# Two layers of a hybrid gMLP, S5 and pooling backbone on one core: where modulation loads, first splits, lag rows and outputs stand in the queues

## The chip, the core and the metric

One core of one Trainium2 chip runs the whole program, and the metric is device microseconds of one execution. In the profile PE is TensorE (PEld its weight loads), DVE VectorE, ACT ScalarE, POOL GpSimd and SP the engine that only issues DMAs. Each engine works through its instructions in order, and a DMA queue belongs to the engine that issues it. The profile comes from one more execution than the timed ones.

## The reference

There are 512 latent tokens, 256 context tokens, a width of 1024 and two layers. Layer 1 returns latent tokens only. Cut to what matters here:

```python
for i in range(2):
    mod = silu(c) @ w_mod[i] + b_mod[i]          # for c (latent) and c_ctx (context)
    sh1, sc1, g1, sh2, sc2, g2 = split(mod, 6)
    h = rms_norm(x, norm_mix_pre[i]) * (1 + sc1) + sh1
    z = h @ w_in[i]                              # 1280 columns: 512 gMLP, 512 S5, 256 pooling
    a = spatial_gating(z[:, :512])
    s = glu(gelu(d * u + sum over 2 directions of Re(C scan(lam, B u))))   # u = z[:, 512:1024]
    p = pool_mixer(z[:, 1024:])                  # means over 2, 4, 8 and 16 tokens
    x = x + g1 * rms_norm(concat(a, s, p) @ w_out[i], norm_mix_post[i])
    h = rms_norm(x, norm_ffn_pre[i]) * (1 + sc2) + sh2
    x = x + g2 * rms_norm((silu(h @ w_gate[i]) * (h @ w_up[i])) @ w_down[i], norm_ffn_post[i])
```

x starts as the input plus a fixed sine and cosine table. The S5 part has 32 groups of 16 channels and 64 complex states, and runs over context and latent tokens in both directions.

## The kernel before

The work is tiled by 128 tokens (six tiles, of which the first two are context). Products with large weights are made of three: each weight block and each activation is split into a rounded part and a rest (`split`, line 130: ScalarE casts, VectorE subtracts), and `mm3` (line 141) issues rounded by rounded, rounded by rest and rest by rounded. `wblock` (line 134) loads a 512 KB block through SP's queue into one of two buffers `raw` and splits it into `whi` and `wlo`.

*Order.* The program is written as Python generators. A planner places the instructions on the engines: an earlier line has the higher priority, an instruction goes to its engine when the planner's own clock holds it ready, and a buffer is given out when an older tile of its tag is released. `tc.issue_after(ins)` puts the instructions made within its block, on the engine of `ins`, behind `ins`. `tc.high_priority` raises a block.

*Prologue* (lines 1224 to 1299). Small vectors go through ScalarE's queue (`dmas`, lines 1230 to 1250), x and ctx through SP. `first_mod_loads` (192) loads the parts of `w_mod` that layer 0's first shift and scale need, 16 pieces of 512 KB (some as 1 MB), by column quarters j; between its first pieces and the rest `prep_load_rows` (494) loads B as rows and C. For each j `first_mod_sums` (212) forms the sums on TensorE, `first_mod` (221) makes the columns, with the bias in `fbias`, and `to_hT` (339) makes a quarter of the transposed input h in three token pairs and splits it. `ssm_params` (363) is the discretization, a long chain of small VectorE instructions with two ScalarE sines; its last TensorE transposes are on line 441.

*Block preparation* `ssm_prep` (513). For each eight groups (layer 0) or four (layer 1) it makes rotation tables Td, state inputs X, their reversed copy XF (line 597) turned to Ed, outputs Y and their reversed copy (line 629) written as Fd, and the lag matrix Kd (line 674 on). All five are written to device memory through GpSimd's queue. In layer 0 it runs one step at a time (`bgstep`) beside the first weight products; layer 1's runs in the FFN of layer 0.

*Mixing* (853). `z_B` (866) makes the S5 inputs u of 128 channels each, m = 0 to 3. Then `PRE_A` steps of the gMLP product follow, then eight blocks bt of the recurrence. A block has `ssm_UV` (769, products with E), `ssm_rot` (794, two scans on VectorE between two rotations) and `ssm_y` (824, products with T and F). `ssm_FT` (782) loads F, and for every second block T, in eight pieces of 64 KB that are shifted windows of Kd. `ssm_y` writes its result to device memory (`yd`) and at once fetches it back transposed, in four loads. All of these are on SP's queue. Between the blocks `fl` gives steps of the gMLP and pooling products, and `filler` steps of the modulations.

*Modulations.* `mod_rows` (232) forms one 1024-wide part on TensorE: a bias product, then eight steps of one 512 KB load (tag `rawm`, two buffers, SP) and four products. `mod_rows_v` (255) does it on VectorE with accumulators per lane (latent, context), then a bias product and one product per lane. In layer 0's mixing run (0, 3), (0, 4), (0, 2) and (0, 5), the number being the sixth of `w_mod`. In the FFN of layer 0 run layer 1's six by `mod_rows_v`: `filler` (1323) takes one step after an up block and two in a down block, and the rest ahead of the last down part.

Of the kernel before, what the change touches and what calls it, by code (L numbers as in the profile page):

```python
# [84 lines left out]
def tile_backbone(ctx, tc, A, out):  # L85
# [39 lines left out]

    last_v = [None]
# [65 lines left out]
    def first_mod_loads(res):  # L192
# [4 lines left out]
        for (j, m), w in where.items():  # L197
# [5 lines left out]
            else:  # L203
                res[j, m] = []
                for h in range(2):
                    t = wp.tile([128, 4, 256], F32, tag=w, name=nm("wm"), bufs=2)
                    dma(t, A["w_mod"][0, 512 * h:512 * h + 512, c_].rearrange("(t p) c -> p t c", p=128))
# [23 lines left out]

    def mod_rows(l, m, res):
        ps = mdt()
        bm = wp.tile([1, 1024], F32, name=nm("bm"), tag="rawm", bufs=2)
        dma(bm, A["b_mod"][l:l + 1, m * 1024:(m + 1) * 1024])
        for j in range(4):
            mm(ps[32 * j:32 * j + 32, :256], bc(ident[0:1, 0:1], [1, 32]),
               bm[:, 256 * j:256 * j + 256], start=True, stop=False, tile_position=(0, 32 * j))
        for k in range(8):
            raw = wp.tile([128, 1024], F32, name=nm("wm"), tag="rawm", bufs=2)  # L240
            dma(raw, A["w_mod"][l, k * 128:(k + 1) * 128, m * 1024:(m + 1) * 1024])
            for j in range(4):
                mm(ps[32 * j:32 * j + 32, :256], csil[:, 2 * k:2 * k + 32], raw[:, 256 * j:256 * j + 256],
                   start=False, stop=k == 7, tile_position=(0, 32 * j))
            if k % 2 == 1:
                yield
        M = sp.tile([128, 256], F32, tag="M", name=nm("M"), bufs=1)
        S.copy(M, ps[:, :256])
        res.append(M)

# [4 lines left out]
    def mod_rows_v(l, m, res, lanes):  # L255

        accs = [q4([128, 1024], s="macc") for _ in range(lanes)]
        for k in range(8):
            raw = wp.tile([128, 1024], F32, name=nm("wm"), tag="rawm", bufs=2)
            dma(raw, A["w_mod"][l, k * 128:(k + 1) * 128, m * 1024:(m + 1) * 1024])  # L260
# [7 lines left out]
        bm = wp.tile([1, 1024], F32, name=nm("bm"), tag="rawm", bufs=2)  # L268
        dma(bm, A["b_mod"][l:l + 1, m * 1024:(m + 1) * 1024])
        ps = mdt()  # L270
        for j in range(4):
            c_ = slice(256 * j, 256 * j + 256)
            mm(ps[32 * j:32 * j + 32, :256], bc(ident[0:1, 0:1], [1, 32]), bm[:, c_], start=True, stop=False,
               tile_position=(0, 32 * j))
# [1092 lines left out]
```

## Time and profile before

| | us |
|---|---|
| three runs | 1552.45, 1559.03, 2079.58 (median 1559.03) |
| profiled execution | 1553.79 |
| its span, from the first to the last instruction | 1552.0 |
| TensorE busy in it | 1475.9 |

Busy time of a stage says how full an engine is there. A wait counts only where the waiting engine has nothing else, and above all TensorE. The stages of the profiled execution are the prologue to about 66 us, the first products with layer 0's preparation to 160, its recurrence to 285, output projection to 400, FFN to 960, then layer 1: mixing to 1200, FFN to the end.

### The profile page before, as it was taken

Reading aid. Unit: us, or ns where it says so; the run is one execution under the profiler, and the core shown is the slowest. Engines: PE = TensorE matmul, PEld = TensorE weight load, DVE = VectorE, ACT = ScalarE, POOL = GpSimd, SP = SyncE. Lnnn points to the kernel's source line nnn. Section 1 sums busy time; section 2 is a strip of 40 time slices with the busy share of each in tenths; the row PEclk is TensorE's granted clock in tenths of the full one; section 3 lists DMA queues with packets and bytes.
Section 4 is the critical chain, followed back from the end, with each engine's and each line's share of the span. In section 5 each row is a group of like instructions: output and inputs, shape, how many; then the busy total and the mean of one; then the engine's idle time right before and its main releaser. Section 6 shows DMA issues by size and latency. Waiting matters only on the chain.

```text
span 1552.0 us, 22603 instructions
## 1 busy us (share of the span) xinstructions
PE 1475.9 (95%) x8777; PEld 1227.6 (79%) x8777; DVE 841.0 (54%) x1479; ACT 630.7 (41%) x1182; POOL 161.1 (10%) x281
## 2 busy tenths in 40 slices
PE   4899898999999999999999999999988999999996
PEld 3766695888888778888778887899778888888885
DVE  5977864646465676445763336587555332333334
ACT  3778564446323234233222215656454223222222
POOL 1113210012000010000010005211011000000003
PEclk9999999999999999999999999999999999999998
DMA  9788987773334455333674314768474333333332
GB/s 294 246 274 262 306 273 220 254 181 108 92 109 121 138 185 175 111 95 118 209 261 128 95 62 130 235 170 240 112 265 135 95 95 97 99 102 97 96 95 82
DMA packets 219487, 250.68 MB, mean 162 GB/s; under 512 B 41806, under 2 KB 164058, under 8 KB 218868
## 3 DMA queue, kind: packets, MB, share of 16 engines
q1 hardware_dynamic: 209268, 214.26, 45.5%
q0 software_dynamic: 9344, 34.58, 6.4%
q8 instruction: 69, 1.13, 0.3%
q10 hardware_dynamic: 768, 0.40, 0.1%
q14 instruction: 38, 0.31, 0.1%
HBM read 206.76 MB, written 42.43 MB: 161 GB/s over the span
## 4 chain that ended last, share of the span: by engine, by line
PE 81%; DMA 9%; DVE 4%; ACT 3%; POOL 1%; issue 1%; SPq 1%; DVEq 0%; POOLq 0%; ACTq 0%
PE acc L142 20%; PE acc L144 19%; PE acc L143 19%; PE aux L144 4%; PE aux L142 4%; PE aux L143 4%; PE pr L147 3%; PE md L147 3%; PE aux L147 2%; DMA F<-Fd 2%; DMA raw<-in_w_out_dram 1%; DMA wm<-in_w_mod_dram 1%; DVE w L132 1%; DMA raw<-in_w_in_dram 1%; PE acc L147 1%
## 5 line engine op out<-in xcount | busy, mean ns | idle before, releaser
L142 PE MATMUL acc<-h,w 128*128 128x512 f32 (+1 forms) x1248 | 430.1, 346 | 1.2 <-ACT w L131 0.8
L144 PE MATMUL acc<-h,w 128*128 128x512 f32 (+1 forms) x1248 | 428.4, 344 | 2.8 <-DVE w L132 2.8
L143 PE MATMUL acc<-h,w 128*128 128x512 f32 (+1 forms) x1248 | 429.5, 345 | 1.5 <-DVE h L356 1.4
L132 DVE TENSOR_TENSOR w<-raw,w 128x1024 fp32r<-128x1024 f32 x190 | 233.0, 1227 | 335.1 <-ACT w L131 332.3
L131 ACT CAST w<-raw 128x1024 fp32r<-128x1024 f32 x190 | 199.3, 1050 | 411.7 <-PE acc L143 231.3
L142 PEld LDWEIGHTS acc<-h,w 128*128 128x128 f32 x1248 | 235.8, 190 | 33.6 <-issue 3.4
L144 PEld LDWEIGHTS acc<-h,w 128*128 128x128 f32 x1248 | 236.1, 189 | 33.1 <-DVE w L132 3.6
L143 PEld LDWEIGHTS acc<-h,w 128*128 128x128 f32 x1248 | 236.3, 189 | 30.8 <-DVE h L356 2.3
L1142 DVE TENSOR_TENSOR fsg<-fsg,acc 128x512 f32<-128x512 f32 (+1 forms) x68 | 39.8, 585 | 159.7 <-PE acc L144 156.8
L144 PE MATMUL aux<-w,act 128*128 128x512 f32 x220 | 86.2, 393 | 0.0
L143 PE MATMUL aux<-w,act 128*128 128x512 f32 x220 | 86.2, 392 | 0.0
L144 PE MATMUL acc<-w,act 128*128 128x512 f32 x220 | 86.0, 391 | 0.0
L143 PE MATMUL acc<-w,act 128*128 128x512 f32 x220 | 85.8, 390 | 0.0
L142 PE MATMUL aux<-w,act 128*128 128x512 f32 x220 | 82.7, 390 | 0.0
L142 PE MATMUL acc<-w,act 128*128 128x512 f32 x220 | 82.5, 392 | 0.0
L266 DVE SCALAR_TENSOR_TENSOR macc<-wm,csil,macc 128x1024 f32<-128x1024 f32 x56 | 70.6, 1278 | 5.5 <-DMA wm<-in_w_mod_dram 5.4
L1143 ACT CAST act<-fsg 128x512 fp32r<-128x512 f32 (+1 forms) x68 | 36.5, 537 | 87.5 <-DVE fsg L1142 87.5
L1141 ACT ACTIVATE fsg<-acc 128x512 f32<-128x512 f32 (+1 forms) x68 | 34.8, 511 | 81.4 <-PE acc L144 81.4
L143 PE MATMUL acc<-w,h 128*128 128x512 f32 (+1 forms) x160 | 55.6, 348 | 1.1 <-DVE w L132 1.1
L147 PE MATMUL md<-wm,csil 128*32 128x256 f32 (+1 forms) x416 | 35.6, 404 | 21.1 <-DMA wm<-in_w_mod_dram 21.1
L144 PE MATMUL acc<-w,h 128*128 128x512 f32 (+1 forms) x160 | 55.2, 345 | 0.0
L142 PE MATMUL acc<-w,h 128*128 128x512 f32 (+1 forms) x160 | 53.9, 354 | 0.0
(370 smaller groups left out, 2322.8 us busy)
## 6 DMA issues: line engine op xcount, KB each, us to landing
wm<-in_w_mod_dram SPq DMA_DIRECT2D x90, 512.0 KB, 4.3
raw<-in_ffn_w_gate_dram SPq DMA_DIRECT2D x44, 512.0 KB, 3.9
raw<-in_ffn_w_up_dram SPq DMA_DIRECT2D x44, 512.0 KB, 3.8
raw<-in_ffn_w_down_dram SPq DMA_DIRECT2D x44, 512.0 KB, 3.8
raw<-in_w_in_dram SPq DMA_DIRECT2D x28, 512.0 KB, 5.0
raw<-in_w_out_dram SPq DMA_DIRECT2D x26, 512.0 KB, 6.9
xt<-xd SPq DMA_DIRECT2D x18, 512.0 KB, 4.9
Ed<-Et POOLq DMA_DIRECT2D x16, 512.0 KB, 4.7
```

The costliest lines, as they stand in the source:

```text
L131: S.copy(hi, raw)
L132: last_v[0] = V.tensor_sub(lo, raw, hi)
L142: PE.matmul(ps, lhi, rhi, start=start, stop=False, skip_group_check=True)
L143: PE.matmul(ps, lhi, rlo, start=False, stop=False, skip_group_check=True)
L144: return PE.matmul(ps, llo, rhi, start=False, stop=stop, skip_group_check=True)
L147: return PE.matmul(ps, lhsT, rhs, start=start, stop=stop, skip_group_check=True, **k)
L266: V.scalar_tensor_tensor(accs[r], raw, c_, accs[r], op0=ALU.mult, op1=ALU.add)
L1141: S.activation(sg[:, :n], p1[:, :n], AF.Silu)
L1142: V.tensor_mul(sg[:, :n], sg[:, :n], p2[:, :n])
L1143: S.copy(act[0][:, fl, o:o + n], sg[:, :n])
```

## The change

The diff, cut to its core (in both modulation functions the loads change from `dma`, SP, to `dmap`, GpSimd):

```diff
-    def wblock(src, shape, tags=("whi", "wlo")):
+    def wblock(src, shape, tags=("whi", "wlo"), after=()):
...
-        split(raw, hi, lo)
+        with ExitStack() as st:
+            for ins in after[:2]:
+                st.enter_context(tc.issue_after(ins.ins))
+            split(raw, hi, lo)
...
+    def bias_rows(l, m, lanes):
+        M = sp.tile([128, 256], F32, tag="M", name=nm("M"), bufs=1)
+        GP.memset(M, 0.0)
+        for r in range(lanes):
+            dmap(M[r:128:32, :], A["b_mod"][l, m * 1024:(m + 1) * 1024].rearrange("(j c) -> j c", j=4))
+        return M
...
     def mod_rows(l, m, res):
...
+        for k in range(0, 8, 2):
+            raw = [wp.tile([128, 1024], F32, name=nm("wm"), tag="rawm", bufs=2) for _ in range(2)]
+            for kk in range(2):
+                dmap(raw[kk], A["w_mod"][l, (k + kk) * 128:(k + kk + 1) * 128, m * 1024:(m + 1) * 1024])
+            if k == 2:
+                M = bias_rows(l, m, 2)
+            for kk in (1, 0):
+                for j in range(4):
+                    mm(ps[32 * j:32 * j + 32, :256], csil[:, 2 * (k + kk):2 * (k + kk) + 32],
+                       raw[kk][:, 256 * j:256 * j + 256], start=k == 0 and kk == 1, stop=k == 6 and kk == 0,
+                       tile_position=(0, 32 * j))
+            yield
+        V.tensor_add(M, ps[:, :256], M)
...
+    def prep_load_C(l):
         Cr = q4([128, 2, 4, 2, 64], s="Cr")
         for i, s_ in enumerate(("re", "im")):
-            dma(raw[32 * i:32 * i + 32], A[f"ssm_b_{s_}"][l].rearrange("k g a b -> g k (a b)"))
             for k in range(2):
                 dma(Cr[:, i, :, k, :], A[f"ssm_c_{s_}"][l, k].rearrange("(b g) h p -> (g h) b p", b=4))
-        return raw, Cr
+        return Cr
+
+    def prep_load_rows(l, raw):
+
+        for i, s_ in enumerate(("re", "im")):
+            dma(raw[32 * i:32 * i + 32], A[f"ssm_b_{s_}"][l].rearrange("k g a b -> g k (a b)"))
+        return raw
...
-        for i in range(2):
-            ps = prt()
+        with ExitStack() as st:
+            for ins in ssm["h", 2] if bufs is not None else ():
+                st.enter_context(tc.issue_after(ins.ins))
+            for i in range(2):
...
-                S.copy(XF[0:64, i], X[0:64, i, :, ::-1, :])
+                (GP.tensor_copy if l == 0 else S.copy)(XF[0:64, i], X[0:64, i, :, ::-1, :])
...
+                Kw[l, blk] = dr.tile([8, 16, 8, 128], F32, name=nm("Kw"))
...
-                S.copy(XF[64:128, i], Y[64:128, i, :, ::-1, :])
+                (GP.tensor_copy if l == 0 else S.copy)(XF[64:128, i], Y[64:128, i, :, ::-1, :])
...
+            if g0 % 8 + ng == 8:
+                for s in range(8):
+                    dmap(Kw[l, blk][s].rearrange("h g c -> g h c"), Kd[l, blk][:, :, 16 * (7 - s):16 * (7 - s) + 128])
...
-            for s in range(8):
-                dma(T_[16 * s:16 * s + 16], Kd[l, blk][:, :, 16 * (7 - s):16 * (7 - s) + 128]
-                    .rearrange("g h c -> h g c"))
+            dma(T_.rearrange("p g c -> p (g c)"), Kw[l, blk].rearrange("s h g c -> (s h) (g c)"))
...
-        dma(yd.rearrange("t h g c -> (t h) (g c)"), yt)
-        for g in range(4):
-            p0 = 64 * (bt % 2) + 16 * g
-            dma(g_[p0:p0 + 16, :, c0:], yd[:, :, g, :].rearrange("t h c -> h t c"))
+        ins = dma(yd.rearrange("t h g c -> (t h) (g c)"), yt)
+
+        def back():
+            for g in range(4):
+                p0 = 64 * (bt % 2) + 16 * g
+                dma(g_[p0:p0 + 16, :, c0:], yd[:, :, g, :].rearrange("t h c -> h t c"))
+
+        with tc.issue_after(ins.ins):
+            for f_ in late:
+                f_()
+        late[:] = [back]
+        if bt == 7:
+            late.clear()
+            back()
...
-            hi, lo = wblock(w_in[:, :, 512 + 128 * m:640 + 128 * m], [128, 8, 128])
+            hi, lo = wblock(w_in[:, :, 512 + 128 * m:640 + 128 * m], [128, 8, 128],
+                            after=ssm["h", min(m + 2, 3)] if l == 0 else ())
...
-        dmas(vrow[r0:r0 + w], s_)
-    dmas(dmask, A["k_dm"])
-    dmas(par01, A["k_par"])
+        dmap(vrow[r0:r0 + w], s_)
...
-    BC0 = prep_load_rows(0, pzb[0:64, 4:6])
+    brows = prep_load_rows(0, pzb[0:64, 4:6])
     drain(loads)
     next(params)
+    with tc.issue_after(ssm["wmod"].ins):
+        BC0 = brows, prep_load_C(0)
+        dma(dmask, A["k_dm"])
+        dma(par01, A["k_par"])
...
-    bg.append(ssm_prep(0, *BC0, bufs=pzb))
-    bgstep(6)
...
-            first_mod_sums(j, wm0, fps)
+            with ExitStack() as st:
+                if j == 0:
+                    st.enter_context(tc.issue_after(ssm["turned"].ins))
+                first_mod_sums(j, wm0, fps)
...
+            ssm["h", j] = last_s[0], last_v[0], last_h[0]
+    bg.append(ssm_prep(0, *BC0, bufs=pzb))
+    bgstep(6)
...
-            mods = chain(mod_cols(l, 3, 3, None), mod_cols(l, 4, 2, 16 + 8 * l), mod_G(l, 2), mod_G(l, 5))
+            mods = chain(mod_cols(l, 3, 3, None), mod_cols(l, 4, 2, 16 + 8 * l), mod_G(l, 2))
...
-            mq = chain(mod_cols(1, 0, 1, None, 2), mod_cols(1, 1, 0, 8, 2), mod_cols(1, 3, 3, None, 1),
+            mq = chain(mod_G(0, 5, 2), mod_cols(1, 0, 1, None, 2), mod_cols(1, 1, 0, 8, 2), mod_cols(1, 3, 3, None, 1),
```

Beside this, the memset and the four bias loads of `fbias` move behind the vector loads, onto GpSimd's queue. `mod_rows_v` takes its bias from `bias_rows` after its eighth step, so its first lane's product starts the sum in PSUM and VectorE adds the bias. `ssm["wmod"]` is the last load of `first_mod_loads`, `ssm["turned"]` the last transpose on line 441, and `ssm["h", j]` holds the last ScalarE, VectorE and TensorE instruction of quarter j of h.

## Rows read from the trace of the kernel before

**Rows 1.** The page: the span, and busy time, share and instructions of TensorE.

```profile
span 1552.0 us, 22603 instructions
PE 1475.9 (95%) x8777; PEld 1227.6 (79%) x8777; DVE 841.0 (54%) x1479; ACT 630.7 (41%) x1182; POOL 161.1 (10%) x281
```

**Rows 2.** Busy us by stage: PE, PEld, DVE, ACT, POOL (instructions); clock, DMA share, GB/s.

```profile
39.00:66.00 27.00, 21.92 (x250) 19.16 (x250) 26.61 (x68) 20.15 (x42) 2.54 (x5) 0.87 0.69 207
66.00:160.00 94.00, 94.00 (x684) 66.20 (x683) 71.73 (x230) 73.69 (x160) 21.35 (x41) 1.00 0.87 281
160.00:200.00 40.00, 33.51 (x266) 27.58 (x264) 35.13 (x69) 20.84 (x54) 11.88 (x13) 0.91 0.96 308
220.00:285.00 65.00, 58.25 (x441) 42.89 (x441) 34.74 (x48) 30.27 (x58) 2.63 (x4) 0.95 0.79 239
400.00:820.00 420.00, 420.00 (x2445) 345.57 (x2444) 248.75 (x406) 132.56 (x229) 27.86 (x50) 1.00 0.48 151
1040.00:1110.00 70.00, 64.75 (x492) 59.82 (x491) 46.18 (x81) 37.14 (x79) 6.93 (x10) 0.98 0.72 208
```

**Rows 3.** Timeline of TensorE, the first weight product: start, us, engine, line, operation, tiles.

```profile
66.82 0.36 PE L142 MATMUL acc<-h,w 128*128 128x256 f32 x1
```

**Rows 4.** Timelines of ScalarE and SP in the prologue.

```profile
16.50 0.26 ACT L402 ACTIVATE pwork<-pwork 128x64 f32<-128x64 f32 x1 [12.30 <-DMA cr<-in_sgu_b_dram]
...
17.93 1.94 SPq L500 DMA_DIRECT2D Cr<-in_ssm_c_re_dram  x2
22.04 0.92 SPq L500 DMA_DIRECT2D Cr<-in_ssm_c_im_dram  x2
```

**Rows 5.** VectorE's groups by line, 39 to 66 us: busy us, mean ns, idle before.

```profile
L356 DVE TENSOR_TENSOR h<-h,h 128x512 fp32r<-128x512 f32 x9 | 6.1, 681 | 0.0
L355 DVE CAST h<-h 128x512 fp32r<-128x512 f32 x9 | 3.8, 420 | 0.3 <-ACT h L351 0.2
L132 DVE TENSOR_TENSOR w<-raw,w 128x1024 fp32r<-128x1024 f32 x2 | 2.4, 1216 | 0.0
```

**Rows 6.** Timeline of TensorE, a bias, a k step and what follows.

```profile
171.93 0.63 PE L147 MATMUL md<-bm,ident 1*32 1x256 f32 x8
172.49 0.64 PE L147 MATMUL md<-wm,csil 128*32 128x256 f32 x8
173.06 1.58 PE L147 MATMUL aux<-zslot,E 128*128 128x96 f32 x12
```

**Rows 7.** TensorE's waits from 160 to 285 us: in total, times, longest.

```profile
PE md L147 <- DMA wm<-in_w_mod_dram: 6.1, 5, 2.2
PE pr L147 <- DMA pc<-in_k_pc_dram: 2.5, 1, 2.5
PE aux L147 <- DMA E<-Ed: 1.8, 1, 1.8
```

**Rows 8.** Timeline of SP in the recurrence of layer 0.

```profile
152.90 8.04 SPq L789 DMA_DIRECT2D T<-Kd  x8
188.35 3.37 SPq L841 DMA_DIRECT2D wk<-yd  x4
```

**Rows 9.** Groups by line and form: GpSimd's and ScalarE's copies; Kd's issue, and its landing.

```profile
L798 POOL COPY wk<-PT 128x384 f32<-128x384 f32 x16 | 19.6, 1226 | 94.8 <-DVE wk L807 94.6
L679 POOL DMA_DIRECT2D Kd<-klag x4 | 2.2, 557 | 13.9 <-DVE klag L669 13.8
...
L597 ACT COPY pz<-pz 64x1024 f32<-64x1024 f32 x8 | 8.0, 1043 | 0.3 <-DVE pz L550 0.3
...
Kd<-klag POOLq DMA_DIRECT2D x4, 120.0 KB, 5.3
```

**Rows 10.** VectorE's group of one modulation sum.

```profile
L266 DVE SCALAR_TENSOR_TENSOR macc<-wm,csil,macc 128x1024 f32<-128x1024 f32 x56 | 70.6, 1278 | 5.5 <-DMA wm<-in_w_mod_dram 5.4
```

**Rows 11.** Timeline of GpSimd, two of the copies of line 798.

```profile
164.10 0.50 POOL L798 COPY wk<-PT 128x384 f32<-128x384 f32 x1 [7.73 <-DVE wk L807]
184.86 5.00 POOL L798 COPY wk<-PT 128x384 f32<-128x384 f32 x1 [8.35 <-DVE wk L807]
```

More of the change, by code (lines that the diff above doesn't have):

```diff
@@ L206, in first_mod_loads @@
                     t = wp.tile([128, 4, 256], F32, tag=w, name=nm("wm"), bufs=2)
-                    dma(t, A["w_mod"][0, 512 * h:512 * h + 512, c_].rearrange("(t p) c -> p t c", p=128))
+                    ssm["wmod"] = dma(t, A["w_mod"][0, 512 * h:512 * h + 512, c_].rearrange("(t p) c -> p t c", p=128))
                     res[j, m] += [t[:, k] for k in range(4)]
@@ L230, in first_mod @@
                                bc(vecT[:, ks][:, None, :], [128, 2, 2]), op0=ALU.add, op1=ALU.mult)
+    def bias_rows(l, m, lanes):
[4 more added lines that the diff above has]
+        return M
     def mod_rows(l, m, res):
         ps = mdt()
[L234 to L248, printed above, removed]
+        for k in range(0, 8, 2):
[11 more added lines that the diff above has]
+        V.tensor_add(M, ps[:, :256], M)
         res.append(M)
@@ L259, in mod_rows_v @@
             raw = wp.tile([128, 1024], F32, name=nm("wm"), tag="rawm", bufs=2)
-            dma(raw, A["w_mod"][l, k * 128:(k + 1) * 128, m * 1024:(m + 1) * 1024])
+            dmap(raw, A["w_mod"][l, k * 128:(k + 1) * 128, m * 1024:(m + 1) * 1024])
             for r in range(lanes):
@@ L267, in mod_rows_v @@
             yield
-        bm = wp.tile([1, 1024], F32, name=nm("bm"), tag="rawm", bufs=2)
-        dma(bm, A["b_mod"][l:l + 1, m * 1024:(m + 1) * 1024])
+        M = bias_rows(l, m, lanes)
         ps = mdt()
[L271 to L274, printed above, removed]
         for r in range(lanes):
@@ L277, in mod_rows_v @@
                 mm(ps[32 * j:32 * j + 32, :256], osel[:, 31 - r:63 - r], accs[r][:, 256 * j:256 * j + 256],
-                   start=False, stop=r == lanes - 1, tile_position=(0, 32 * j))
-        M = sp.tile([128, 256], F32, tag="M", name=nm("M"), bufs=1)
-        S.copy(M, ps[:, :256])
+                   start=r == 0, stop=r == lanes - 1, tile_position=(0, 32 * j))
+        V.tensor_add(M, ps[:, :256], M)
         res.append(M)
@@ L440, in ssm_params @@
                 V.tensor_copy(dup, R[:, i:i + 1, :].to_broadcast([128, 2, 64]))
-                PE.transpose(ps[:, 128 * (i - b0):128 * (i - b0) + 128],
-                             dup.rearrange("p a b -> p (a b)"), ident)
+                ssm["turned"] = PE.transpose(ps[:, 128 * (i - b0):128 * (i - b0) + 128],
+                                             dup.rearrange("p a b -> p (a b)"), ident)
             pv = ps[:, :128 * (b1 - b0)].rearrange("p (i l k g) -> p i l k g", l=2, k=2, g=G)
@@ L529, in ssm_prep @@
              .rearrange("p a (g h) -> p a g h", h=16))
-        for i in range(2):
-            ps = prt()
-            for blk in range(4):
-                PE.transpose(ps[:, 128 * blk:128 * blk + 128], Cr[:, i, blk].rearrange("p k q -> p (k q)"), ident)
-            S.activation(Cc[:, i], ps, AF.Copy, scale=(1.0, -1.0)[i])
+        with ExitStack() as st:
+            for ins in ssm["h", 2] if bufs is not None else ():
+                st.enter_context(tc.issue_after(ins.ins))
+            for i in range(2):
+                ps = prt()
+                for blk in range(4):
+                    PE.transpose(ps[:, 128 * blk:128 * blk + 128], Cr[:, i, blk].rearrange("p k q -> p (k q)"), ident)
+                S.activation(Cc[:, i], ps, AF.Copy, scale=(1.0, -1.0)[i])
         yield
@@ L1232, in tile_backbone @@
     dmas(jrow, A["k_j"][:, None, :])
-    GP.memset(fbias, 0.0)
-    for m in range(2):
-        for hf in range(2):
-            c0 = 64 * m + 32 * hf
-            src = A["b_mod"][0:1, 1024 * m:1024 * m + 1024].rearrange("o (j h c) -> o h j c", j=4, h=2)[:, hf]
-            dmas(fbias[c0:c0 + 2], src.to_broadcast([2, 4, 128]))
     for n_, r0, w in (("norm_mix_pre", 0, 16), ("norm_ffn_pre", 16, 16), ("glu_b", 32, 8),
@@ L1247, in tile_backbone @@
             s_ = a_.rearrange("l (k p) -> (l k) p", p=128)
-        dmas(vrow[r0:r0 + w], s_)
-    dmas(dmask, A["k_dm"])
-    dmas(par01, A["k_par"])
+        dmap(vrow[r0:r0 + w], s_)
+    GP.memset(fbias, 0.0)
+    for m in range(2):
+        for hf in range(2):
+            c0 = 64 * m + 32 * hf
+            src = A["b_mod"][0:1, 1024 * m:1024 * m + 1024].rearrange("o (j h c) -> o h j c", j=4, h=2)[:, hf]
+            dmap(fbias[c0:c0 + 2], src.to_broadcast([2, 4, 128]))
     for h in range(2):
```

10 lines of the change are left out of this document (5 added, 5 removed).

## Prediction

> **What bounds the kernel now.** I read the page first, then busy time by stage, then the timelines and waits of the stages where TensorE is not full. The page shows TensorE busy for 1475.9 of 1552.0 us [rows 1]: the end is set by TensorE's work and by the gaps in it. The stages say where the gaps are [rows 2]. From 66 to 160 us, and in the FFN of layer 0 (400 to 820), TensorE is busy all the time: there only less TensorE work helps. Ahead of that, TensorE reaches the first weight product at 66.82 [rows 3], while VectorE is busy for 26.61 of the 27 us from 39 to 66 [rows 2]: until 66 it is VectorE that sets the pace. In the recurrence of layer 0 TensorE lacks 6.49 us from 160 to 200 and 6.75 from 220 to 285, at a mean granted clock of 0.91 and 0.95 (full, 2.4 GHz, with stretches at the half level, 1.2, where TensorE had waited), which costs another 0.09 x 40 = 3.6 and 0.05 x 65 = 3.3 us of full-clock work: 20.1 us lost there. The same stage of layer 1 (1040 to 1110) lacks 5.25 us. The DMA share is 0.79 to 0.96 in layer 0's recurrence.
>
> **The change part by part.** Durations are of the profiled execution (span 1552.0, run 1553.79); the sum starts from 1553.8. The median of the three runs shown is 1559.03, 5 us above; I expect a repeat near the profiled one.
>
> 1. *The start.* ScalarE's first sine waits 12.30 us behind its own queue of small loads [rows 4]; six vector loads and four bias loads go to GpSimd's queue, so the discretization chain on VectorE and the norms can start earlier, by those 12.30 us at most. GpSimd has idle time there; its ten issues, at the 0.557 us of a Kd issue [rows 9], are 5.6 us beside the loads of x. SP issues the C blocks between 17.93 and 22.96 [rows 4], ahead of most of w_mod; they move behind it, so the last quarter of w_mod can land up to 5.0 us earlier. The prologue's h work is 6.1 + 3.8 us on VectorE between 39 and 66, the two weight splits 2.4 [rows 5]; the other 14.3 of the 26.6 us are block preparation and small columns. Splits and preparation now stand behind h, on both engines by an added order. What queues behind a split is the first products; who waits is TensorE. The first weight product can come between 0 and 2.4 + 14.3 = 16.7 us earlier. I take 6.2: 5.0 for the C loads and one 1.2 us split. I don't take more, because the preparation put back is due again before the recurrence starts, and VectorE has 94 - 71.7 = 22.3 us left in 66 to 160 to hold it. Sum -6.2, ends 0 and -16.7.
>
> 2. *TensorE work.* One k step of a modulation on TensorE starts at 172.49, the next work at 173.06: 0.57 us; a bias (171.93 to 172.49) is 0.56 [rows 6]. The change drops the bias products of ten modulations, adding a memset and one or two small loads on GpSimd and a VectorE add in place of a ScalarE copy. Six of the ten are in the FFN, two in 66 to 160, where TensorE is full: 8 x 0.56 = -4.5. The modulation (0, 5) moves to the FFN as VectorE sums: 2 lanes x 0.57 = +1.1 us of TensorE there, and 16 sums at 1.278 us = 20.4 us of VectorE [rows 10], which is busy 248.75 of 420 there [rows 2]: room for it, 0 to +5, taken 0. The queue now ends the up and down steps with ten leftover steps instead of one; they run under the last down part. Sum -3.4, ends -4.5 and +1.6.
>
> 3. *The recurrence of layer 0.* There TensorE waits 6.1 us for w_mod, 2.5 for the pooling constants and 1.8 for E [rows 7]. All three come off SP's queue, which is in order: eight T loads hold it for 8.04 us at 152.90, and the four fetches of yd at 188.35 for 3.37, because they wait for yd to land [rows 8]. Four such T groups become one load each; fetches stand behind the next block's write and no longer wait; w_mod goes to GpSimd's queue; and 4.2 MB of w_mod (8 loads of 512 KB), some 17 us at the 239 GB/s of 220 to 285 [rows 2], leave for a stage with a DMA share of 0.48. The modulation that leaves also takes 8 x 0.57 + 0.56 = 5.1 us from TensorE, and two more biases 1.1. What is late next is VectorE's rotation, whose blocks are a chain, and the last fetch, which is unchanged. Ends: 0, and -(20.1 + 6.2) = -26.3. I take the waits named, 10.4, and half of the 6.9 us of clock: -13.9, and nothing for the TensorE work, since it lies in a stage that has gaps.
>
> 4. *The recurrence of layer 1.* The same T loads and fetches; lost are 5.25 us and 0.02 x 70 = 1.4 of clock. Ends 0 and -6.7; taken -4.0.
>
> 5. *GpSimd's load.* XF's two halves, 8 + 8 copies of 64x1024 in layer 0, leave ScalarE at 1.043 us each (the first eight in [rows 9]). The trace has no such copy on GpSimd; its 128x384 copies take 1.226 us on average [rows 9], 0.50 where nothing is in the way and 5.00 in one case [rows 11]. By length, 1024 for 384, that is 1.33 us at the 0.50 and 3.27 at the mean. At 1.33 the chain of preparation grows by 16 x 0.29 = 4.6 us, at 3.27 by 16 x 2.23 = 35.7; ScalarE gets back 16.7. Of Kw's eight copies per block, the first waits for Kd to land, 5.3 us, and each takes 0.557 to issue [rows 9]: up to 5.3 + 4.5 = 9.8 us of GpSimd per block, behind which stand the next block's XF copies, its writes and the w_mod pairs; TensorE waits for the last and for XF's turned tiles. Three blocks are in the way, ends 0 and +29. A Kd row is written late in a block, when the next block's first XF is due, so part of it can be met. I take +4.0 in all, nearest to the row of 0.50, because most of what preparation issues on GpSimd has slack up to the recurrence; ends -4, where only ScalarE's relief counts, and +36. By GpSimd's busy time, 21.35 of 94 us in 66 to 160 [rows 2], the change adds 16 x 1.33 = 21.3, three Kw groups 13.4 and some 16 w_mod issues 9: 65 of 94, still below full.
>
> The row of 5.00 us [rows 11] lies in the stretch where VectorE, with its products and sums of two tiles each, is busy 35.13 of 40 us [rows 2]. The Trainium skill (SBUF — State Buffer, section Who interferes with whom) has a rule that speaks against this edit: a VectorE instruction with two inputs in SBUF and a GpSimd instruction that reads SBUF lock each other out, and the later one waits for the whole of the other. The trace agrees in that row, ten times the 0.50 beside it. By the rule alone the copies would cost the +36, and the sum would be 1562; by the row of 0.50 it is the one below.
>
> Sum: -6.2 - 3.4 - 13.9 - 4.0 + 4.0 = -23.5, so **1530 us**.
>
> **The rivals.**
> - *More of the gaps close.* The first product comes the full 16.7 us earlier, the recurrence gives 20.1, layer 1 6.7, GpSimd costs nothing: -16.7 - 3.4 - 20.1 - 6.7 = -46.9, 1507 us. For it: every wait named in the recurrence comes from the queue that is emptied. Against it: VectorE is busy 35.13 of 40 us from 160 to 200 [rows 2], so the rotation soon sets the pace.
> - *The gains are hidden.* The preparation's end, not the first product, sets when the recurrence starts, and w_mod waits for GpSimd instead of SP: the wait stays and only changes its queue. Then 3.4 and 4.0 remain: 1546 us. For it: TensorE is already full from 66 to 160, so an earlier start only brings forward its fillers. Against it: TensorE's waits lie in the recurrence, behind SP.
> - *Slower: GpSimd's copies sit on the chain of preparation.* At 3.27 us a copy the chain grows by 35.7 us, the start's gain is swallowed by it, and 3.4 + 4.0 stay: 1553.8 + 35.7 - 7.4 = 1582 us. It decides from the copy's mean at which 16 x (t - 1.043) eats the sum of the other terms, 27.5: t = 2.76 us. For it: the mean of the GpSimd rows, and VectorE's load of 71.73 in 94 us. Against it: ScalarE, busy 73.69 of 94 [rows 2], gets time back, and the chain has TensorE's fillers beside it. The rule cited in part 5 gives the reason why it could come so.
> - *The change doesn't do what it says:* an order that the planner gives differently from the source (it places by priority, so a moved line need not move an instruction). That falls into the hidden case.
>
> **How the numbers follow.** Forecast (1514 to 1546): 0.50. More gaps close (1490 to 1514): 0.22. Hidden (1546 to 1560): 0.18. Slower (above 1560): 0.10, of which 0.06 above 1585. The bound of 2%, about what a measurement of this kernel can tell from no change, is 31 us: 1523 and 1585. Faster: 0.22 and 0.18 of the forecast's own half-range below 1523, 0.40; slower 0.06; same 0.54. The range leaves out 0.1 on either side: 1503 to 1560. The likeliest case's own range is 1514 to 1546.
>
> **What would show it.** Right: the first weight product before 62; C loads after the last w_mod issue; no TensorE wait on w_mod or the pooling constants between 160 and 285; one T issue per pair of blocks; granted clock near 1.0 from 160 to 285; XF copies near 1.3 us. Wrong: XF copies near 3 us, TensorE or the turned tiles waiting for them; TensorE waiting for w_mod on GpSimd's queue; VectorE without a gap and TensorE waiting for splits in the FFN of layer 0.

## The result, and the profile after

The changed kernel takes 1566.8 us (median) where the kernel before took 1554.5 in the same measurement. The ratio, which leaves out one run of the kernel before that was far slower than the rest (2079.58 us), is 1.0092 with a 95% interval of [1.0068, 1.0116]; the two medians by themselves give 1.0079. It is slower by 0.9%, less than the 2% bound. Forecast was 1530, range 1503 to 1560.

The page of the kernel after, against [rows 1]: TensorE is as busy as before, so the 13.6 us by which the profiled execution is longer are gaps. But it is as busy with 128 matmuls fewer: the mean granted clock over the span is 0.972, before it was 0.987.

```profile
span 1565.6 us, 22441 instructions
PE 1475.3 (94%) x8649; PEld 1235.8 (79%) x8649; DVE 872.7 (56%) x1505; ACT 613.8 (39%) x1158; POOL 280.1 (18%) x477
```

The windows of [rows 2], of the kernel after (columns as there):

```profile
39.00:66.00 27.00, 25.44 (x299) 21.97 (x299) 26.19 (x68) 20.52 (x49) 9.93 (x15) 1.00 0.76 227
66.00:160.00 94.00, 84.00 (x557) 58.59 (x556) 67.46 (x194) 49.02 (x110) 42.89 (x64) 0.96 0.80 257
160.00:200.00 40.00, 28.00 (x182) 20.53 (x183) 25.79 (x54) 17.55 (x48) 20.39 (x26) 0.54 0.80 252
220.00:285.00 65.00, 58.66 (x491) 51.32 (x491) 43.09 (x84) 35.88 (x83) 15.98 (x28) 0.94 0.75 242
400.00:820.00 420.00, 419.28 (x2447) 347.20 (x2446) 257.86 (x420) 134.77 (x232) 70.47 (x126) 1.00 0.47 141
1040.00:1110.00 70.00, 66.80 (x504) 63.54 (x504) 58.06 (x99) 40.13 (x92) 8.23 (x14) 0.96 0.74 230
```

Until 66 us TensorE gained (25.44 busy for 21.92). Then, from 66 to 160, where it had been full, it lacks 10 us; from 160 to 200 it lacks 12, and in these 40 us the granted clock is 0.54, near the half level of 1.2 GHz, after that waiting. VectorE and ScalarE are not the fuller for it: they have *less* to show from 66 to 160 (67.46 for 71.73, 49.02 for 73.69; up to 16.7 us of the latter are the copies that ScalarE gave away). Everybody waits.

Three milestones tell where. They are the first product of a rotation on VectorE: the first and the eighth of layer 0, and the first of layer 1. Kernel before, timeline of VectorE (start, us, engine, line, operation, tiles, idle time before it):

```profile
158.01 0.96 DVE L801 TENSOR_TENSOR wk<-zslot 128x768 f32<-128x768 f32 x1 [3.23 <-ACT zslot L779]
...
243.55 0.97 DVE L801 TENSOR_TENSOR wk<-zslot,tab 128x768 f32<-128x768 f32 x1
...
1013.32 0.95 DVE L801 TENSOR_TENSOR wk<-zslot 128x768 f32<-128x768 f32 x1
```

The same three, kernel after, and ahead of them the wait that matters (read below):

```profile
114.39 0.41 DVE L478 TENSOR_TENSOR tmp<-Cc,PT 128x256 f32<-128x256 f32 x1
119.16 1.23 DVE L133 TENSOR_TENSOR w<-raw,w 128x1024 fp32r<-128x1024 f32 x1 [4.36 <-ACT w L132]
129.91 1.22 DVE L133 TENSOR_TENSOR w<-raw,w 128x1024 fp32r<-128x1024 f32 x1 [9.53 <-ACT w L132]
...
133.13 0.39 DVE L479 TENSOR_TENSOR pz<-Cc,PT 128x256 f32<-128x256 f32 x1
...
180.46 0.96 DVE L815 TENSOR_TENSOR wk<-zslot 128x768 f32<-128x768 f32 x1 [2.91 <-ACT zslot L795]
...
261.73 0.95 DVE L815 TENSOR_TENSOR wk<-zslot,tab 128x768 f32<-128x768 f32 x1
...
1029.78 0.95 DVE L815 TENSOR_TENSOR wk<-zslot 128x768 f32<-128x768 f32 x1
```

| stretch | before | after | difference |
|---|---|---|---|
| to the first rotation | 158.01 | 180.46 | +22.45 |
| first to eighth rotation | 85.54 | 81.27 | -4.27 |
| to the first rotation of layer 1 | 769.77 | 768.05 | -1.72 |
| from there to the end | 538.7 | 535.8 | -2.9 |

Behind the first rotation each stretch is shorter, as forecast. All of the loss against the kernel before, and more, lies ahead of it. The block preparation, which stands ahead of the recurrence in the source, ends late too: its last write of Ed is issued 26.9 us later (GpSimd, kernel before and after):

```profile
149.91 0.62 POOL L612 DMA_DIRECT2D Ed<-Et  x1
```

```profile
176.85 0.53 POOL L624 DMA_DIRECT2D Ed<-Et  x1 [0.42 <-ACT klag L681]
```

Yet the first weight product, of [rows 3], comes 9.4 us earlier:

```profile
57.43 0.36 PE L146 MATMUL acc<-h,w 128*128 128x256 f32 x1
```

The rows of VectorE above show one place where the preparation falls behind. Line 478 (114.39) and line 479 (133.13) are two neighbouring steps of one block's preparation. Between them in VectorE's order stand the splits of two weight blocks; each waits for ScalarE's cast, and that for the weight. ScalarE and SP say why the weight is late:

```profile
118.07 1.05 ACT L132 CAST w<-raw 128x1024 fp32r<-128x1024 f32 x1 [4.04 <-DMA raw<-in_w_in_dram]
...
128.83 1.04 ACT L132 CAST w<-raw 128x1024 fp32r<-128x1024 f32 x1 [8.63 <-DMA raw<-in_w_in_dram]
...
110.58 0.39 SPq L137 DMA_DIRECT2D raw<-in_w_in_dram  x1
116.75 4.62 SPq L902 DMA_DIRECT2D zslot<-zd  x8
121.47 0.98 SPq L137 DMA_DIRECT2D raw<-in_w_in_dram  x2
```

The second load is issued at 121.47, behind eight fetches of z. So VectorE stands idle for 4.36 + 9.53 us with the next step of preparation behind the splits, although that step (line 479) reads the same Cc and PT as line 478, which has run: an order that is bad for the times that came. Over the whole stretch from 66 to 180 us VectorE's waits for splits (total, times, longest) grew from 4.1 us in the kernel before to 19.2:

```profile
DVE w L132 <- ACT w L131: 4.1, 3, 2.6
```

```profile
DVE w L133 <- ACT w L132: 19.2, 6, 9.5
```

TensorE's waits from 160 to 285 us, against [rows 7] (total, times, longest): those for the pooling constants are gone, those for w_mod smaller; new are the preparation's (klag is the lag matrix, pz the buffer of X, XF and Y).

```profile
PE pr L151 <- DVE klag L682: 6.1, 1, 6.1
PE md L151 <- DMA wm<-in_w_mod_dram: 4.2, 2, 2.9
PE pr L151 <- DVE pz L562: 4.0, 1, 4.0
...
PE pr L736 <- DMA wk<-yd: 2.4, 1, 2.4
```

GpSimd's groups of the XF copies from 40 to 200 us, which [rows 9] did not have:

```profile
L609 POOL COPY pz<-pz 64x1024 f32<-64x1024 f32 x8 | 11.7, 1490 | 24.5 <-DVE pz L562 24.5
L642 POOL COPY pz<-pz 64x1024 f32<-64x1024 f32 x8 | 10.6, 1350 | 0.2
```

They take 1.42 us on average: close to the 1.33 that the forecast took, far from the 3.27 of its slower rival.

### The profile page after: what moved, and what is told of

The parts are those of the page before. It is cut to its first block, busy times and chain, and to the rows that moved or that the text cites. A ratio compares the mean times of both kernels' runs of the same rounds, so it can differ in the third digit from the quotient of the medians.

```text
span 1565.6 us, 22441 instructions
## 1 busy us (share of the span) xinstructions
PE 1475.3 (94%) x8649; PEld 1235.8 (79%) x8649; DVE 872.7 (56%) x1505; ACT 613.8 (39%) x1158; POOL 280.1 (18%) x477
## 4 chain that ended last, share of the span: by engine, by line
PE 79%; DMA 6%; ACT 5%; DVE 5%; issue 2%; SPq 2%; POOL 1%; DVEq 0%; ACTq 0%; POOLq 0%
PE acc L146 19%; PE acc L147 19%; PE acc L148 19%; PE aux L146 4%; PE aux L148 4%; PE aux L147 4%; PE aux L151 4%; PE pr L151 3%; PE md L151 2%; DMA wm<-in_w_mod_dram 1%; DMA raw<-in_w_in_dram 1%; ACT w L132 1%; DVE w L133 1%; DMA zd<-zslot 1%; DMA wk<-yd 1%
## 5 line engine op out<-in xcount | busy, mean ns | idle before, releaser
L1167 DVE TENSOR_TENSOR fsg<-fsg,acc 128x512 f32<-128x512 f32 (+1 forms) x68 | 39.8, 585 | 146.9 <-PE acc L148 144.0
L277 DVE SCALAR_TENSOR_TENSOR macc<-wm,csil,macc 128x1024 f32<-128x1024 f32 x70 | 88.8, 1292 | 13.8 <-DMA wm<-in_w_mod_dram 13.8
L271 POOL DMA_DIRECT2D wm<-in_w_mod_dram x56 | 30.9, 552 | 351.6 <-DVE macc L277 174.4
L1223 POOL TENSOR_TENSOR m<-m,G 128x512 f32<-128x512 f32 x10 | 16.3, 1655 | 351.6 <-ACT jk L1051 351.6
L146 PE MATMUL acc<-w,h 128*128 128x512 f32 (+1 forms) x160 | 54.6, 355 | 7.3 <-ACT ast L716 7.2
L147 PE MATMUL acc<-w,h 128*128 128x512 f32 (+1 forms) x160 | 55.6, 348 | 1.1 <-DVE w L133 1.1
```

The source lines that it names most:

```text
L146: PE.matmul(ps, lhi, rhi, start=start, stop=False, skip_group_check=True)
L147: PE.matmul(ps, lhi, rlo, start=False, stop=False, skip_group_check=True)
L271: dmap(raw, A["w_mod"][l, k * 128:(k + 1) * 128, m * 1024:(m + 1) * 1024])
L277: V.scalar_tensor_tensor(accs[r], raw, c_, accs[r], op0=ALU.mult, op1=ALU.add)
L1167: V.tensor_mul(sg[:, :n], sg[:, :n], p2[:, :n])
L1223: (GP if h == 0 else V).tensor_tensor(mt[:, i, c_], mt[:, i, c_], Gs[1 if i < 2 else 0][:, c_], op=ALU.mult)
```

## The experiments

Ratios are to the kernel before, measured beside each run.

**First theory.** A: the start's new order puts preparation behind splits that wait for late weights. B: GpSimd's queue (XF, Kw, w_mod) delays the preparation.

*e1: the start undone.*

```diff
+    bg.append(ssm_prep(0, *BC0, bufs=pzb))
+    bgstep(6)
     hh = [bigt([128, 8, 768], F32R, "h") for _ in range(2)]
...
-    bg.append(ssm_prep(0, *BC0, bufs=pzb))
-    bgstep(6)
...
-            for ins in ssm["h", 2] if bufs is not None else ():
-                st.enter_context(tc.issue_after(ins.ins))
...
-                            after=ssm["h", min(m + 2, 3)] if l == 0 else ())
+                            )
...
-                    st.enter_context(tc.issue_after(ssm["turned"].ins))
```

> The changed kernel with its start order undone: block preparation is placed ahead of h again, and the two weight splits and C's transposes have no added order; everything else of the change stays. Theory A (the new start order makes the first products run ahead of a preparation that then stands behind splits that wait for late weight loads; the recurrence cannot start before the preparation ends): the last Ed write comes back from 176.9 us to about 150, the first rotation from 180 to about 160, and the time falls by 12 to 25 us, to 1542 to 1555. Theory B (GpSimd's queue, with XF copies, Kw issues and w_mod waits, delays the preparation): the last Ed write stays above 165 and the time stays at 1560 to 1572.

1562.6 us, 1.0088 [1.0062, 1.0114]; last Ed write at 180.3, first rotation at 179.5. A falls as the cause by itself. From 110 to 136 us VectorE waits only 1.5 us for splits here, but from 66 to 180 still 12.8: the preparation falls behind in more places than the one shown. The first rotation even comes ahead of the last Ed write, which is thus a mark of how late the preparation is, and not the gate itself.

*e2: XF on ScalarE again.*

```diff
-                (GP.tensor_copy if l == 0 else S.copy)(XF[0:64, i], X[0:64, i, :, ::-1, :])
+                S.copy(XF[0:64, i], X[0:64, i, :, ::-1, :])
...
-                (GP.tensor_copy if l == 0 else S.copy)(XF[64:128, i], Y[64:128, i, :, ::-1, :])
+                S.copy(XF[64:128, i], Y[64:128, i, :, ::-1, :])
```

> The changed kernel with the XF copies of layer 0 back on ScalarE, nothing else. Theory A: the preparation still ends late, 1560 to 1570. Theory B, in its form that the copies on GpSimd are to blame: the last Ed write comes at least 10 us earlier and the time falls by 8 us or more, below 1559.

1538.5 us, 0.9930 [0.9909, 0.9951]: these two lines turn the change from a loss of 0.9% into a gain of 0.7%. The last Ed writes are at 150.7 instead of 176.9. The milestones, with these writes ahead:

```profile
150.74 1.14 POOL L624 DMA_DIRECT2D Ed<-Et  x2
...
158.06 0.96 DVE L815 TENSOR_TENSOR wk<-zslot 128x768 f32<-128x768 f32 x1 [2.10 <-ACT zslot L795]
...
241.50 0.95 DVE L815 TENSOR_TENSOR wk<-zslot,tab 128x768 f32<-128x768 f32 x1
...
1000.27 0.95 DVE L815 TENSOR_TENSOR wk<-zslot 128x768 f32<-128x768 f32 x1
```

The changed kernel's profiled span is 28.7 us longer than e2's: 22.4 of them lie ahead of the first rotation and 9.3 between the eighth and layer 1; in the two other stretches it is 3.0 shorter. Seen from TensorE, 16.7 of the 28.7 are the same 8649 matmuls being busy longer (1475.3 us at a mean granted clock of 0.972, in e2 at 0.982):

```profile
PE 1458.6 (95%) x8649; PEld 1225.4 (80%) x8649; DVE 863.7 (56%) x1505; ACT 632.7 (41%) x1176; POOL 255.5 (17%) x461
```

*e3: no Kw copies, T in eight loads.*

```diff
-            if g0 % 8 + ng == 8:
-                for s in range(8):
-                    dmap(Kw[l, blk][s].rearrange("h g c -> g h c"), Kd[l, blk][:, :, 16 * (7 - s):16 * (7 - s) + 128])
...
-            dma(T_.rearrange("p g c -> p (g c)"), Kw[l, blk].rearrange("s h g c -> (s h) (g c)"))
+            for s in range(8):
+                dma(T_[16 * s:16 * s + 16], Kd[l, blk][:, :, 16 * (7 - s):16 * (7 - s) + 128]
+                    .rearrange("g h c -> h g c"))
```

> The changed kernel without the Kw copies: T is fetched by eight loads straight from Kd as before, and GpSimd issues no Kw copy. Theory A: 1558 to 1570, since the groups of 4.8 us on GpSimd stand ahead of only one Ed write per block (4 to 8 us back at most, and 8 us per block on SP's queue added). Theory B, in its form that the Kw groups hold Ed, Kd and w_mod: at least 10 us back, 1556 or less.

1564.0 us, 1.0092 [1.0065, 1.0119]. The first rotation came at 161.8 (last Ed write 160.3), 18.7 us earlier than in the changed kernel, but from there to the eighth it took 90.4 us instead of 81.3, so half of the gain was lost by then, and by the median the rest was lost as well. (The profiled run, 1561.4, is the fastest of its seven and 6 us shorter than that of the changed kernel.)

*e4: modulations as before*, both functions taken from the kernel before.

```diff
-            for kk in range(2):
-                dmap(raw[kk], A["w_mod"][l, (k + kk) * 128:(k + kk + 1) * 128, m * 1024:(m + 1) * 1024])
...
+            dma(raw, A["w_mod"][l, k * 128:(k + 1) * 128, m * 1024:(m + 1) * 1024])
...
-            mods = chain(mod_cols(l, 3, 3, None), mod_cols(l, 4, 2, 16 + 8 * l), mod_G(l, 2))
+            mods = chain(mod_cols(l, 3, 3, None), mod_cols(l, 4, 2, 16 + 8 * l), mod_G(l, 2), mod_G(l, 5))
```

> The changed kernel with the modulations as before: bias by products, w_mod one tile at a time on SP's queue, and (0, 5) back in the recurrence of layer 0. Theory A: the preparation is still late, and the terms that I booked for the modulations come back: 1566 to 1580. Theory B, in its form that the pairs on GpSimd's queue, which wait for TensorE, hold the preparation's writes: 1550 to 1560.

1569.6 us, 1.0129 [1.0086, 1.0172]. So of B, undone part by part, only the copies are left. But 16 copies that are 1.42 - 1.04 = 0.38 us longer make 6 us, not the 25 of 1.6%. Hence two new theories: B1, the copies themselves (their length, or GpSimd holding VectorE up); B2, the order that the planner writes when they stand on GpSimd.

*e5: the kernel before, with only the XF copies on GpSimd.*

```diff
-                S.copy(XF[0:64, i], X[0:64, i, :, ::-1, :])
+                (GP.tensor_copy if l == 0 else S.copy)(XF[0:64, i], X[0:64, i, :, ::-1, :])
...
-                S.copy(XF[64:128, i], Y[64:128, i, :, ::-1, :])
+                (GP.tensor_copy if l == 0 else S.copy)(XF[64:128, i], Y[64:128, i, :, ::-1, :])
```

> The kernel before with only the XF copies of layer 0 moved to GpSimd. Theory B1 (the copies alone cost the time, wherever GpSimd's queue stands): last Ed write from 149.9 to 165 or later, 1565 to 1580. Theory B2 (they cost it through the order in which VectorE then takes weight splits and preparation, which depends on the rest of the kernel): anything from 1545 to 1580, and the time follows the last Ed write, not the summed length of the copies. A rival, that they cost only together with Kw and w_mod on the same queue: 1548 to 1555.

1575.2 us, 1.0154 [1.0103, 1.0204]; last Ed write at 173.1, first rotation at 174.7. The edit costs the same without Kw and w_mod on that queue.

*e6: XF on ScalarE, each copy made twice.*

```diff
                 S.copy(XF[0:64, i], X[0:64, i, :, ::-1, :])
+                if l == 0:
+                    S.copy(XF[0:64, i], X[0:64, i, :, ::-1, :])
```

> The changed kernel with the XF copies on ScalarE, each done twice: the chain of preparation is longer by 16 x 1.04 = 16.7 us against the run with single copies (1538), which is more than the 16 x 0.36 = 5.8 us that the copies on GpSimd are longer. Theory B1 (length of the copies in the chain): 1555 or more, at least two thirds of the way to the changed kernel's 1566. Theory B2 (order): the added length is partly hidden, 1540 to 1552.

1548.9 us, 0.9986 [0.9964, 1.0008]: 16.7 us more copying in the chain cost 0.6%, where the 6 us more on GpSimd cost 1.6%. That speaks against length, but doesn't settle it: the planner was free here too, and in the traces e6 differs from e2 in the order of its instructions as well.

*e7: GpSimd's copies, with three fillers queued behind preparation on VectorE* (`ssm["X", b]` and `ssm["Y", b]` are here late VectorE instructions of X and Y of block b).

```diff
-            for _ in range((0,0,3,3,3,3,3,3)[bt] if lat_only else FPB):
-                next(fl, None)
+            for n in range((0,0,3,3,3,3,3,3)[bt] if lat_only else FPB):
+                with ExitStack() as st:
+                    if l == 0 and bt == 0:
+                        st.enter_context(tc.issue_after(ssm[(("Y", 2), ("X", 3), ("Y", 3))[n]].ins))
+                    next(fl, None)
```

> The changed kernel, XF copies on GpSimd, with one added order on VectorE and nothing else: the three fillers of the first recurrence step (a weight split of the gMLP projection first) are queued behind the preparation steps of the third and fourth block. Theory B2 (order): VectorE's standstill from 114 to 130 us goes, the last Ed write comes before 162 and the time falls to 1540 to 1553. Theory B1 (the copies' length, or GpSimd holding VectorE): the last Ed write stays at 170 or later and the time above 1560.

1560.5 us, 1.0056 [1.0034, 1.0078], between the two: VectorE's wait for splits fell from 13.9 to 3.4 us in the stretch (110 to 136), but a wait of 6.6 for klag, whose last products TensorE began only at 120.19, came in its place, the last Ed write stayed at 177.5 and the first rotation moved only to 172.8. Inconclusive: one engine's order was not enough.

*e8: one copy of each pair on either engine.*

```diff
-                (GP.tensor_copy if l == 0 else S.copy)(XF[0:64, i], X[0:64, i, :, ::-1, :])
+                (GP.tensor_copy if l == 0 and i else S.copy)(XF[0:64, i], X[0:64, i, :, ::-1, :])
...
-                (GP.tensor_copy if l == 0 else S.copy)(XF[64:128, i], Y[64:128, i, :, ::-1, :])
+                (GP.tensor_copy if l == 0 and i else S.copy)(XF[64:128, i], Y[64:128, i, :, ::-1, :])
```

> The changed kernel with one of the two XF copies of each pair on ScalarE and one on GpSimd, side by side. By the length of the chain it is shorter than either (1.4 us per pair where ScalarE alone takes 2.1): theory B1 wants 1530 to 1540. Theory B2 (order) does not bind it to the chain: 1535 to 1566, going with the last Ed write.

1564.4 us, 1.0091 [1.0061, 1.0122], with a chain that is the shortest of all by the copies' lengths: against B1. Here the first rotation was earlier (165.5, last Ed write 160.9) and the loss came later, again from an order. Timeline of SP,

```profile
254.97 0.34 SPq L852 DMA_DIRECT2D yd<-zslot  x1
255.41 1.39 SPq L857 DMA_DIRECT2D zslot<-yd  x1
256.90 0.38 SPq L772 DMA_DIRECT2D pc<-in_k_pc_dram  x1
```

and TensorE's longest wait from 225 to 305 us (total, times, longest):

```profile
PE pr L151 <- DMA pc<-in_k_pc_dram: 10.8, 2, 9.3
```

The pooling constants, which wait for nothing, stand behind a store of yd that waits for its block, and TensorE stands 10.8 us for them.

**The order by itself.** To part the order from the copies, the order of one program was written out, engine by engine, and forced on another, only the place of the 16 copies being left free.

```diff
+def as_ordered(tc):
+    traced = {i.name: i for i in tc.nc.cur_bb.bb.instructions}
+    for packed in ORDER.values():
...
+                tc.add_manual_dep(i, last.name, mybir.DependencyInfo(
+                    mybir.DependencyClass.NoSync, mybir.DependencyReason.DATA), reason="issue_after")
...
         tile_backbone(tc, args, outs[0])
+        as_ordered(tc)
```

*p1: copies on GpSimd, order of e2.*

> XF copies on GpSimd, and every engine takes all its other instructions in exactly the order that the program with the copies on ScalarE has (that order is written out and forced; only the place of the 16 copies in GpSimd's queue is left to the planner). If the order is the cause (theory B2): near the 1538 of that program, 1534 to 1548. If the copies on GpSimd are slow for the chain or hold VectorE (theory B1): near the changed kernel, 1558 or more.

*p2: copies on ScalarE, order of the changed kernel.*

> The reverse: XF copies on ScalarE, and every engine takes all its other instructions in exactly the order of the changed kernel. Theory B2 (order): the time stays with the changed kernel, 1556 to 1568, with VectorE's standstill from 114 to 130 us still there. Theory B1 (the copies): it falls to 1536 to 1548.

p1 took 1536.3 us, 0.9899 [0.9879, 0.9919]; p2 1563.5, 1.0076 [1.0056, 1.0096]. The order was taken over as meant: in the traces all 8649 matmuls of p1 stand in e2's order and all of p2 in the changed kernel's, while of e2 and the changed kernel only 7570 stand in the same place. The time goes with the order and not with the engine of the copies. So do the wait and the milestone. VectorE's wait for splits from 110 to 136 us, in p1 and then in p2, whose 13.9 us are also the changed kernel's figure (4.36 + 9.53):

```profile
DVE w L235 <- ACT w L234: 2.4, 1, 2.4
```

```profile
DVE w L236 <- ACT w L235: 13.9, 3, 7.2
```

and the first rotation, in p1 and in p2:

```profile
156.54 0.96 DVE L917 TENSOR_TENSOR wk<-zslot 128x768 f32<-128x768 f32 x1 [1.29 <-ACT zslot L897]
```

```profile
176.97 0.96 DVE L918 TENSOR_TENSOR wk<-zslot 128x768 f32<-128x768 f32 x1 [2.78 <-ACT zslot L898]
```

*p3: the kernel before, copies on GpSimd, its own order forced.*

> The kernel before with its XF copies on GpSimd, every other instruction on every engine forced into the order of the kernel before. If order alone made this edit cost 1.5% when the planner was free: 1546 to 1556, no difference from before. If the copies do cost the kernel before by themselves: 1562 or more.

1549.1 us, 0.9987 [0.9962, 1.0012], where the planner, left free with the same edit, had made 1.0154 of it (e5). B2 holds there too.

**What the other parts are worth.** Each was undone on e2, the planner free.

*e9: e2 with the start undone* (the diffs of e1 and e2).

> Copies on ScalarE and, on top, the start order undone (preparation ahead of h, no added order for splits and C). What the start part is worth where the copies don't spoil it: if my term of 6.2 us holds, 1538 + 6 = 1544; if the earlier first products are lost again before the recurrence, as in the changed kernel, 1536 to 1541.

1527.2 us, 0.9842 [0.9823, 0.9862], a miss on the other side: in this pair the start's order *costs* 0.9% (the moved loads of the vectors and of C stay moved). Without it the first rotation comes at 146.1, though the first product comes at 64.1 instead of 56.8. It beats both kernels, by 1.6% that before. Its milestones:

```profile
146.06 0.96 DVE L814 TENSOR_TENSOR wk<-zslot 128x768 f32<-128x768 f32 x1 [0.29 <-ACT zslot L794]
...
228.79 0.95 DVE L814 TENSOR_TENSOR wk<-zslot,tab 128x768 f32<-128x768 f32 x1
...
990.49 0.95 DVE L814 TENSOR_TENSOR wk<-zslot 128x768 f32<-128x768 f32 x1
```

*p4: copies on GpSimd, order of e9.*

> The kernel of e9 (start order undone) with XF copies on GpSimd, every other instruction in the order that e9 has with the copies on ScalarE. Order theory: 1522 to 1532, as e9. If the copies cost something in a schedule with fewer gaps: 1535 or more. The same edit with the planner free (e1) measured 1562.6.

1535.9 us, 0.9901 [0.9866, 0.9936], where e1, the same edit with a free order, had 1.0088. Most of it is order again; but 0.6% stays (the intervals just part), so in a tight schedule the copies do cost something. With the copies on GpSimd the start's order is worth nothing either way: p4, without it, has 0.9901, p1, with it, 0.9899.

*e10: e2 without Kw* (the diff of e3).

> Copies on ScalarE and, on top, T fetched by eight loads per two blocks from Kd, with no Kw copies on GpSimd. If the single load of T is worth what I booked for it in both recurrences (about 4 to 8 us): 1542 to 1546. If the Kw groups cost GpSimd's queue as much as they give SP's: 1536 to 1540.

1545.6 us, 0.9964 [0.9949, 0.9979]: the single load is worth 0.3%. It is a trade: without Kw the first rotation comes 11 us earlier (146.9), and from there to the eighth it takes 91.0 us for 83.4.

*e11: e2 with the modulations as before* (the functions of e4).

> Copies on ScalarE, and the modulations as before (bias products, w_mod on SP's queue, (0, 5) in the recurrence of layer 0). By my terms (3.4 for TensorE's work and 6 to 7 of the 13.9 for w_mod's waits and its clock) 1538 + 10 = 1548; if they were worth nothing, 1538; with the order moving as well, 1535 to 1560.

1551.7 us, 1.0000 [0.9982, 1.0017]: this part is worth 0.7%.

*e12: e2 with every output fetched at once.*

```diff
-        with tc.issue_after(ins.ins):
-            for f_ in late:
-                f_()
-        late[:] = [back]
-        if bt == 7:
-            late.clear()
-            back()
+        back()
```

> Copies on ScalarE, and the outputs of each block fetched at once as before. Eight fetch groups that hold SP's queue for about 2 to 3 us each, in the recurrence of layer 0: 1542 to 1550 if SP's queue sets the pace there; 1536 to 1540 if something else does.

1547.5 us, 0.9980 [0.9959, 1.0001]: worth 0.5%. These three runs, like e9, had a free planner, so each holds its own order's luck as well as the part.

## Why the prediction was wrong, step by step

**Part 1, the start (-6.2): wrong, this step failed first.** The first half worked: ScalarE's first sine, which had waited 12.30 us, starts at 9.59 instead of 16.50, and the first product came 9.4 us earlier. But the C loads, booked at 5.0, didn't bring it: with the loads moved and the order undone the first product is at 67.17 in e1 and at 64.11 in e9 (before 66.82). Most of it took the order of splits and preparation, booked at 1.2. What failed is the sentence that the preparation put back finds room because VectorE "has 94 - 71.7 = 22.3 us left". Idle time on an engine that takes its work in order is room only for what stands next in that order. In the kernel after VectorE is idle for 26.5 of these 94 us and the preparation is late all the same, behind splits whose weights had not landed. Three pairs of runs part the start's order from the rest, and in none of them does it gain: the changed kernel beside e1 (1.0092 and 1.0088) and p1 beside p4 show no difference, e2 beside e9 +0.9%, some 13 us the wrong way. No run undoes the moved loads by themselves.

**Part 2 (-3.4) and part 3 (-13.9): right in kind, too large for the kernel as it ran.** From the first to the eighth rotation the changed kernel gains 4.3 us, and 1.7 to layer 1, 6.0 of the 17.3 booked; in e2 it is 2.1 and 11.0. The half of the clock's loss that part 3 took back didn't come: the granted clock fell from 0.91 to 0.54 in 160 to 200 and stayed at 0.94 for 0.95 in 220 to 285 (in e2 it is 0.79 and 1.00). The modulations, the late fetch and the single load are worth 0.7, 0.5 and 0.3%: together 1.5%, 23 us, against the 17.3 booked for parts 2 and 3 and the 4.0 of part 4. Of the waits named, those for w_mod fell from 6.1 to 4.2 us and those for the constants went; that others (klag, pz, yd) would follow on them was not priced.

**Part 4 (-4.0): near.** From the first rotation of layer 1 to the end, all that follows included, the gain is 2.9 us; from 1040 to 1110 TensorE lacks 3.2 us where it lacked 5.25, at a clock of 0.96 for 0.98.

**Part 5 (+4.0): the copy's price was right, the edit's was not.** 1.42 us against 1.33 taken, in part by luck: 1.33 was worked out for an undisturbed copy, and such a pair took 2.02, 1.01 each (last section). I priced the edit by length, "At 1.33 the chain of preparation grows by 16 x 0.29 = 4.6 us", in an order that I held to be fixed. The edit changed the order of the other instructions on every engine, and that cost 1.6% (e2 against the changed kernel; p1 and p2 show that it was the order). This is the step that turned the sign.

**The rivals.** The hidden case named the right gate, "the preparation's end, not the first product, sets when the recurrence starts", but I let that gate only stay or come earlier; it moved 22.5 us the other way. The slower rival had the right place and the wrong reason: it wanted copies of 2.76 us or more. The remark on the planner (a moved line need not move an instruction) is true, and its reverse decided: an edit that moves no line moves instructions. I had priced that at nothing. The rule of the Trainium skill that was weighed is taken up in the last section.

What stays open: why the planner writes the worse order when the copies stand on GpSimd. Seven programs that had them there under a free planner (the changed one, e1, e3, e4, e5, e7 with its one added order, e8 with half of them) took 1.0056 to 1.0154, the six with ScalarE's copies (e2, e6, e9 to e12) 0.9842 to 1.0000. That the planner takes such a copy for longer than it is would fit; it was not tried.

## What to carry to other kernels

Where a planner writes the order, price an edit twice: by its duration in the old order, and by what it does to the order, of which the trace of before tells nothing; then, if it comes out badly, force the one order on the other program before believing that the edited instruction is slow. To find the loss, take a milestone that everything must pass (here the first rotation) and look, on each engine that takes its work in order, for a wait with ready work behind it. Earlier first products were worth nothing here, where the next gate depended on something else, and they had been paid for with exactly that work.

## What the runs showed of the hardware

GpSimd's copies do make VectorE's instructions with two inputs longer, and VectorE's make the copies longer. Single rows of the changed kernel show both (GpSimd's copies in pairs). The pair at 177.43 takes 2.02 us; VectorE stands idle through nearly all of it. The second copy of the pair at 79.28 is under way when a split begins at 80.33, and the split takes 2.05 us instead of some 1.22. Into the pair at 111.80 falls a split that keeps its 1.21 (at 112.33), and the pair takes 3.90:

```profile
79.28 2.01 POOL L609 COPY pz<-pz 64x1024 f32<-64x1024 f32 x2 [4.09 <-DVE pz L562]
...
111.80 3.90 POOL L609 COPY pz<-pz 64x1024 f32<-64x1024 f32 x2 [1.70 <-DVE pz L562]
...
177.43 2.02 POOL L642 COPY pz<-pz 64x1024 f32<-64x1024 f32 x2
```

```profile
80.33 2.05 DVE L133 TENSOR_TENSOR w<-raw,w 128x1024 fp32r<-128x1024 f32 x1 [0.92 <-ACT w L132]
...
112.33 1.21 DVE L133 TENSOR_TENSOR w<-raw,w 128x1024 fp32r<-128x1024 f32 x1
```

The 14 weight splits from 40 to 180 us (busy us and mean ns behind the bar; same order, copies on ScalarE in e2 and on GpSimd in p1) read, in e2:

```profile
L133 DVE TENSOR_TENSOR w<-raw,w 128x1024 fp32r<-128x1024 f32 x14 | 17.0, 1217 | 7.2 <-ACT w L132 7.2
```

and in p1:

```profile
L235 DVE TENSOR_TENSOR w<-raw,w 128x1024 fp32r<-128x1024 f32 x14 | 20.1, 1439 | 5.0 <-ACT w L234 5.0
```

VectorE's busy time over the span grows by 6 to 13 us for the 16 copies (863.7 to 870.0 from e2 to p1, 862.9 to 876.3 from e9 to p4). The Trainium skill (SBUF — State Buffer, section Who interferes with whom) says that a VectorE instruction with two SBUF inputs and a GpSimd instruction that reads SBUF contend, and that the one issued later waits for the whole of the other. The single rows agree, with 0.83 us more for the split and 1.88 for the pair; but over all 16 copies the mean stayed at 1.42 us, and in three of four orders this cost the kernel nothing that can be measured (p1 beside e2, p3 beside the kernel before, the changed kernel beside p2), in the tightest 0.6% (p4 beside e9).
